# Tying every engine queue of a planned decoder trunk to the order of its own list scheduler

## The chip, the cores and the metric

The kernel runs on one core of one Trainium2 chip. The metric is device time in microseconds (us) of that core, as the median of the runs shown. A core has five engines that each take instructions from a queue of their own, in order: PE (TensorE, matrix products), DVE (VectorE), ACT (ScalarE), POOL (GpSimd) and SP (SyncE, which here only issues DMAs).

## The reference

Two consecutive decoder layers are computed for 256 prompt tokens and 8 sample tokens (one decoding step each), with shared weights in float32. Per layer:

```
u    = rms_norm(x)
proj = u @ w_in                      # columns: attention q,k,v | SSM z,x,B,C,dt | mLSTM q,k,v,o,i,f
att  = sliding-window attention      # window 128, sinks, partial rotary
y    = Mamba-2 SSD scan              # causal conv, chunked scan, gate, grouped norm
h    = mLSTM                         # matrix memory, per-head norm, output gate
x    = x + concat(att, y, h) @ w_out
x    = x + square(relu(rms_norm(x) @ w_up)) @ w_down
```

After both layers there is a final RMSNorm. Besides the two outputs the caches and states of every mixer are returned (the last keys and values, conv rows, SSM states, mLSTM memories). d_model is 2048 and the MLP is 8192 wide.

## The kernel before

**Tiling.** Activations lie transposed: channels on 128 partitions, the 264 tokens along the free axis. Every weight matrix is cut into groups of 128 output columns, and a group into halves of 8 x 128 rows (`half`, line 517). A half is one DMA of 512 KB into `raw` (3 buffers), a rounding to fp32r on ACT (`hi`), the remainder `raw - hi` on DVE (`lo`), and 24 matmuls of 128x264 into a PSUM tile `acc` (2 buffers): 8 times hi by the two parts of the activations (named `uh` and `ul` for the normed input), in two bundles of 8, and then a bundle of 8 lo by `uh`. There are 43 groups for w_in, 32 for w_out (of one half each), 64 for w_up and 64 for w_down in each layer.

**Stages.** A layer first runs the input projection. When a group is complete, DVE takes it out of `acc` (the evacuation) and the mixers' work on it begins: gates, rotary (`rope`, line 680), attention (`att_prompt`, 727), convolution, SSD, the eight SSM states of the samples, mLSTM (`mlstm`, 1059) and the memories of the samples. That work is spread over DVE, ACT, POOL and small matmuls into the PSUM tags `ms` and `sg`, and lies beside the weight halves of later groups. Then w_out and the MLP (`mlp`, 1306) follow, which are nearly nothing but weight halves.

**What sets the order.** The program text does not issue instructions. Each call makes a `Node` (`record`, 191), with a price in us from a formula for each engine (`price`, 228); calls inside `with pr.bundle()` (183) on one engine become a single node. At the end `issue` (258) runs a list scheduler over all nodes. It works out a due time for each node by going backwards (line 282 takes `AHEAD` = 6 us off the due times of weight splits), then moves forward in time: for each engine it looks at the nodes whose inputs are written and whose buffers have room, takes the one that can start first, and among those that can start within 0.08 us the one of the best `rank` (378). On PE small products go before weight bundles. On the others `kind` 0 goes first, which is every node that touches the tags `acc`, `ra` or `ac` (the evacuations and the short chains behind them); the rest go by due time. A node's successor on the same engine counts as ready when the node ends. A load that depends on nothing is held until `EARLY` = 30 us before it is due (289). Where DVE and POOL overlap, the later one is made dearer by 0.6 of the overlap, and of at most its own cost (351). The chosen node is handed on at once by `emit` (383), which takes a physical buffer and calls the real engine method, so that all instructions of the profile carry line 398.

The calls that `emit` makes go to the Tile framework. It adds the waits between engines, and it has a scheduler of its own behind that, which takes the order of the calls as a preference, and need not keep it.

**Places that the prediction speaks of.** In `mlstm` the keys of four heads are turned in one bundle, after the evacuation of four groups by `m_evac` (1046):

```
kp = ms_tile([P, 4, P])
with pr.bundle():
    for h in range(4):
        pe.transpose(kp[:, h], mk[:, h, cs], ident)
```

In `att_prompt` the function `scores` (737) makes one bundle of a mask product and two or four products of `qT` (tag `prod`) with the keys. In `rope` the evacuation into an `ra` tile is followed by a shuffle into an `ac` tile on DVE, two POOL products and a DVE sum. `n0s` (1083) is a small load for the mLSTM of the samples, and `wfin` (1361) holds the gains of the final norm, first used in `last_block` (1339) at the end of the last layer. The stores `C_p` and `n_p` (1116, 1117) follow each other on SP.

Of the kernel before, what the change touches and what calls it, by code (L numbers as in the profile page):

```python
# [32 lines left out]
class Store:  # L33


    def __init__(self, prog, pool, shape, dt, tag, name):
        self.prog, self.pool, self.shape, self.dt, self.tag, self.name = prog, pool, tuple(shape), dt, tag, name
        self.free = int(np.prod(shape[1:]))
        self.real = None
        self.log = []  # L40
        self.users = set()
# [107 lines left out]


_REGIONS = {}


class Node:
# [3 lines left out]
class Program:  # L158
# [4 lines left out]
    EARLY = 30.0  # L163
    LOOSE = ("ms", "sg", "ra", "ac", "eA", "eB")

    def __init__(self, nc):
        self.nc = nc
        self.nodes, self.open, self.tau, self.slots, self.stores = [], None, 0.0, {}, {}
        self.engines = dict(PE=nc.tensor, DVE=nc.vector, ACT=nc.scalar, POOL=nc.gpsimd, SP=nc.sync)
        self.pe, self.vec, self.act, self.pool = [Engine(self, e) for e in ("PE", "DVE", "ACT", "POOL")]  # L170
        self.sync = Engine(self, "SP")
        self.is_weight = False
# [210 lines left out]
    def emit(self, n):  # L383
        for s in n.uses:
            if s.real is not None:
                continue
            slots = self.slots[s.tag]
            k = min((x[1], i) for i, x in enumerate(slots) if x[0] is None)[1]
            slots[k][0], slots[k][1] = s, 0.0
            s.slot = slots[k]  # L390
            s.real = s.pool.tile(list(s.shape), s.dt, name=s.name, tag=f"{s.tag}{k}", bufs=1)
        eng = self.engines[n.eng]

        def real(a):
            return a.real() if isinstance(a, View) else a

        for method, args, kw in n.calls:
            getattr(eng, method)(*[real(a) for a in args], **{k: real(a) for k, a in kw.items()})  # L398


class Engine:
# [9 lines left out]
@with_exitstack  # L411
def trunk(ctx, tc, I, O):
    nc = tc.nc
    pr = Program(nc)
    vec, act, pool, pe, sync = pr.vec, pr.act, pr.pool, pr.pe, pr.sync
    tt, stt, ts = vec.tensor_tensor, vec.scalar_tensor_tensor, vec.tensor_scalar
    ptt = pool.tensor_tensor
# [1095 lines left out]
```

## Time and profile before

| | |
|---|---|
| median of 3 runs | 2429.03 us (2425.24 to 2429.54) |
| profiled execution, its own time | 2427.1 us |
| its span, first to last instruction | 2425.3 us |
| mean granted TensorE clock | 0.985 |
| PE busy | 2341.6 us (97%) |
| DVE busy | 1515.9 us (63%) |
| ACT busy | 1098.1 us (45%) |
| POOL busy | 434.0 us (18%) |
| weight loads | 748 of 512 KB, 3.7 to 3.8 us each to landing |

The busy time of an engine is the union of its instructions, so an engine is idle for the rest of the span. Matmuls overlap one another in the records: one of 128x264 is recorded as about 0.285 us while the next starts 0.12 us after it. A wait is idle time of an engine that a semaphore ended, and it is put down to the instruction that released it. The first layer's mixers lie at about 20 to 372 us, its w_out and MLP up to 1219 us; the second layer's mixers at about 1219 to 1560 us.

### The profile page before, as it was taken

How to read it: one execution, taken by the hardware profiler on the slowest of the kernel's cores; microseconds unless marked ns; L12 is line 12 of the kernel's file. 1: busy time of each engine (PE TensorE's matmuls, PEld its weight loads, DVE VectorE, ACT ScalarE, POOL GpSimd, SP SyncE). 2: the span in 40 equal slices, each digit the busy share in tenths (PEclk: the TensorE clock that was granted, in tenths of full speed). 3: DMA queues.
4: the chain of work that ended last, by engine and by line, in shares of the span. 5: the costliest groups of instructions: out<-in, count | busy, mean ns of one | idle time of the engine just before them, and what ended most of it. 6: DMA issues, size and time to landing. Idle time of an engine off the chain costs nothing.

```text
span 2425.3 us, 46071 instructions
## 1 busy us (share of the span) xinstructions
PE 2341.6 (97%) x18874; PEld 2320.0 (96%) x18874; DVE 1515.9 (63%) x2179; ACT 1098.1 (45%) x1700; POOL 434.0 (18%) x408
## 2 busy tenths in 40 slices
PE   7999898999999999999989979999999999999997
PEld 7998888999999999999989979999999999999997
DVE  7868887754454455455686887977545544544544
ACT  5554444553354344344435544445534434434542
POOL 4314631500000000001331273233000000000023
PEclk9999999999999999999999989999999999999998
DMA  6444755555555555555554466665555555555554
GB/s 235 152 152 139 244 195 166 178 179 183 182 178 182 182 182 180 180 181 182 181 163 128 128 220 178 192 191 182 178 182 180 182 182 178 181 181 183 179 179 131
DMA packets 123475, 432.26 MB, mean 178 GB/s; under 512 B 15744, under 2 KB 18432, under 8 KB 123264
## 3 DMA queue, kind: packets, MB, share of 16 engines
q1 hardware_dynamic: 122688, 428.10, 56.7%
q8 instruction: 149, 2.44, 0.4%
q10 hardware_dynamic: 576, 1.22, 0.1%
q14 instruction: 62, 0.51, 0.1%
HBM read 410.10 MB, written 19.16 MB: 177 GB/s over the span
## 4 chain that ended last, share of the span: by engine, by line
PE 83%; DVE 7%; issue 4%; POOL 3%; DMA 2%; ACT 1%; SPq 0%; DVEq 0%; POOLq 0%; ACTq 0%
PE acc L398 80%; PE ms L398 3%; DVE lo L398 2%; PE sg L398 1%; DMA raw<-in_w_in 1%; DVE m L398 1%; DVE tb L398 1%; POOL S L398 1%; ACT hi L398 1%; POOL tb L398 0%; DMA S<-in_ssm 0%; DVE mw L398 0%; DVE ac L398 0%; POOL ysq L398 0%; DVE lA L398 0%
## 5 line engine op out<-in xcount | busy, mean ns | idle before, releaser
L398 ACT CAST hi<-raw 128x1024 fp32r<-128x1024 f32 x748 | 785.2, 1050 | 1033.7 <-PE acc L398 943.9
L398 DVE TENSOR_TENSOR lo<-raw,hi 128x1024 fp32r<-128x1024 f32 x745 | 949.7, 1275 | 363.9 <-ACT hi L398 359.8
L398 PE MATMUL acc<-uh,hi 128*128 128x264 f32 x3392 | 860.9, 288 | 13.9 <-ACT uh L398 10.3
L398 PE MATMUL acc<-ul,hi 128*128 128x264 f32 x3392 | 854.6, 286 | 2.5 <-DVE ul L398 2.5
L398 PEld LDWEIGHTS acc<-uh,hi 128*128 128x128 f32 x3392 | 643.7, 190 | 15.7 <-ACT uh L398 10.3
L398 PEld LDWEIGHTS acc<-ul,hi 128*128 128x128 f32 x3392 | 645.8, 190 | 5.2 <-DVE ul L398 3.1
L398 PE MATMUL acc<-uh,lo 128*128 128x264 f32 x3392 | 485.6, 286 | 4.5 <-DVE lo L398 4.2
L398 PEld LDWEIGHTS acc<-uh,lo 128*128 128x128 f32 x3392 | 442.9, 189 | 6.4 <-DVE lo L398 5.8
L398 PE MATMUL acc<-hA,hi 128*128 128x264 f32 x1280 | 319.2, 285 | 4.0 <-ACT hA L398 4.0
L398 PE MATMUL acc<-lA,hi 128*128 128x264 f32 x1280 | 319.0, 285 | 0.0
L398 PE MATMUL acc<-hB,hi 128*128 128x264 f32 x1280 | 317.8, 284 | 0.0
L398 PE MATMUL acc<-lB,hi 128*128 128x264 f32 x1280 | 317.6, 284 | 0.0
L398 POOL TENSOR_TENSOR ssq<-xt 128x264 f32<-128x264 f32 x4 | 6.2, 1539 | 1381.4 <-DVE xt L398 1381.4
L398 PEld LDWEIGHTS acc<-hA,hi 128*128 128x128 f32 x1280 | 241.8, 189 | 4.6 <-ACT hA L398 4.3
L398 PEld LDWEIGHTS acc<-lA,hi 128*128 128x128 f32 x1280 | 241.2, 189 | 0.3
L398 PEld LDWEIGHTS acc<-lB,hi 128*128 128x128 f32 x1280 | 241.0, 188 | 0.0
L398 PEld LDWEIGHTS acc<-hB,hi 128*128 128x128 f32 x1280 | 240.8, 188 | 0.0
L398 DVE TENSOR_TENSOR xt<-acc,xt 128x264 f32<-128x264 f32 x192 | 82.9, 432 | 241.9 <-PE acc L398 241.8
L398 PE MATMUL acc<-hA,lo 128*128 128x264 f32 x1280 | 181.0, 283 | 0.0
L398 PE MATMUL acc<-hB,lo 128*128 128x264 f32 x1280 | 180.5, 283 | 0.0
L398 DVE SCALAR_TENSOR_TENSOR ra<-acc,rb 128x264 f32<-128x264 f32 x128 | 55.4, 433 | 197.7 <-PE acc L398 197.6
L398 PEld LDWEIGHTS acc<-hA,lo 128*128 128x128 f32 x1280 | 165.6, 188 | 0.0
(308 smaller groups left out, 1817.5 us busy)
## 6 DMA issues: line engine op xcount, KB each, us to landing
raw<-in_w_up SPq DMA_DIRECT2D x256, 512.0 KB, 3.7
raw<-in_w_down SPq DMA_DIRECT2D x256, 512.0 KB, 3.7
raw<-in_w_in SPq DMA_DIRECT2D x172, 512.0 KB, 3.8
raw<-in_w_out SPq DMA_DIRECT2D x64, 512.0 KB, 3.7
S<-in_ssm SPq DMA_DIRECT2D x16, 512.0 KB, 4.5
out_ssm_s<-S SPq DMA_DIRECT2D x16, 512.0 KB, 3.4
S<-in_mC SPq DMA_DIRECT2D x8, 512.0 KB, 4.6
out_C_s<-S SPq DMA_DIRECT2D x8, 512.0 KB, 3.2
```

Of the source, the lines that this page charges most:

```text
L398: getattr(eng, method)(*[real(a) for a in args], **{k: real(a) for k, a in kw.items()})
```

## The change

Each instruction that `emit` traces gets an edge to the instruction traced before it on the same engine. The edge is of a kind that adds no wait on a semaphore; it only forbids the framework's scheduler to put the two in the other order. Nothing else differs: the nodes, the prices, the list scheduler and its result are those of before.

```diff
+ORDER = mybir.DependencyInfo(mybir.DependencyClass.NoSync, mybir.DependencyReason.DATA)
...
-    def __init__(self, nc):
-        self.nc = nc
+    def __init__(self, tc):
+        self.tc, self.nc = tc, tc.nc
+        nc = tc.nc
+        self.last = {}
...
+        traced = self.nc.cur_bb.bb.instructions
+        at = len(traced)
         for method, args, kw in n.calls:
             getattr(eng, method)(*[real(a) for a in args], **{k: real(a) for k, a in kw.items()})
+        for ins in traced[at:]:
+            before = self.last.get(ins.engine)
+            if before is not None:
+                self.tc.add_manual_dep(ins, before, ORDER, reason="order")
+            self.last[ins.engine] = ins.name
...
-    pr = Program(nc)
+    pr = Program(tc)
```

## Rows read from the trace of the kernel before

**Rows 1.** Page, part 1: busy us, share of the span, instructions.
```profile
PE 2341.6 (97%) x18874; PEld 2320.0 (96%) x18874; DVE 1515.9 (63%) x2179; ACT 1098.1 (45%) x1700; POOL 434.0 (18%) x408
```
**Rows 2.** Windows: length, busy us (instructions) by engine, granted clock, DMA share, GB/s.
```profile
20.00:75.00 55.00, 47.65 (x374) 46.47 (x374) 49.36 (x97) 21.10 (x29) 20.07 (x29) 0.95 0.54 173
...
200.00:285.00 85.00, 74.81 (x555) 72.18 (x554) 78.33 (x85) 37.63 (x111) 62.77 (x27) 0.94 0.62 205
...
472.00:1219.00 747.00, 747.00 (x6143) 746.93 (x6142) 394.56 (x472) 330.89 (x400) 36.04 (x31) 1.00 0.59 181
...
1375.00:1470.00 95.00, 81.55 (x609) 77.83 (x608) 82.91 (x89) 40.14 (x112) 61.93 (x26) 0.93 0.65 206
```
**Rows 3.** Waits of PE over the span: total us, times, longest us.
```profile
PE ms L398 <- DVE m L398: 10.0, 2, 5.8
...
PE sg L398 <- DVE prod L398: 8.2, 3, 4.1
...
PE acc L398 <- DVE m L398: 3.6, 4, 1.0
...
PE ms L398 <- POOL ysq L398: 3.2, 2, 2.7
```
**Rows 4.** Timeline of PE, 1441 to 1448.6: start, us, engine, operation [wait before].
```profile
1441.53 0.29 PE L398 MATMUL acc<-ul,hi 128*128 128x264 f32 x1
1441.66 0.49 PE L398 MATMUL ms<-cst,m 128*128 128x128 f32 x3
1447.98 0.48 PE L398 MATMUL ms<-cst,m 128*128 128x128 f32 x1 [5.83 <-DVE m L398]
1448.11 0.57 PE L398 MATMUL acc<-uh,hi 128*128 128x264 f32 x1
```
**Rows 5.** Timeline of PE, 66.5 to 78.
```profile
67.06 0.83 PE L398 MATMUL sg<-tb,prod 128*128 128x128 f32 x6
71.95 0.79 PE L398 MATMUL sg<-tb,prod 128*128 128x128 f32 x2 [4.06 <-DVE prod L398]
...
77.87 0.42 PE L398 MATMUL acc<-ul,hi 128*128 128x264 f32 x1
```
**Rows 6.** Timeline of SP, 0 to 31: DMA issues.
```profile
11.77 0.33 SPq L398 DMA_DIRECT2D n0s<-in_mn  x1
...
29.78 0.42 SPq L398 DMA_DIRECT2D wfin<-in_wfin  x1
```
**Rows 7.** Timeline of DVE, 66.5 to 72 and, last row, 56.5 to 62.5.
```profile
67.05 0.43 DVE L398 TENSOR_TENSOR ra<-acc,rb 128x264 f32<-128x264 f32 x1
67.40 1.22 DVE L398 TENSOR_TENSOR lo<-raw,hi 128x1024 fp32r<-128x1024 f32 x1
...
68.56 0.44 DVE L398 STREAM_SHUFFLE ac<-ra 128x264 f32<-128x264 f32 x1
...
56.93 1.34 DVE L398 SCALAR_TENSOR_TENSOR m<-m 64x264 f32<-64x264 f32 x3
```
**Rows 8.** Timeline of DVE, 1439 to 1448.
```profile
1439.81 5.92 DVE L398 TENSOR_TENSOR lo<-raw,hi 128x1024 fp32r<-128x1024 f32 x2
...
1447.50 0.42 DVE L398 TENSOR_TENSOR m<-acc,rb 128x264 f32<-128x264 f32 x1
```
**Rows 9.** Timeline of POOL, 1438 to 1449.
```profile
1438.54 3.26 POOL L398 TENSOR_TENSOR S<-S,tb 128x1024 f32<-128x1024 f32 x1
```
**Rows 10.** Groups of DVE in 472:1219, then in 200:372: count, busy us, mean ns, idle before.
```profile
L398 DVE TENSOR_TENSOR lo<-raw,hi 128x1024 fp32r<-128x1024 f32 x256 | 312.3, 1220 | 153.7 <-ACT hi L398 153.7
...
L398 DVE TENSOR_TENSOR lo<-raw,hi 128x1024 fp32r<-128x1024 f32 x41 | 70.1, 1713 | 10.2 <-ACT hi L398 9.8 <-ACT lB L398 0.4
```
**Rows 11.** Timeline of DVE, 1466 to 1483.
```profile
1481.17 1.23 DVE L398 TENSOR_TENSOR lo<-raw,hi 128x1024 fp32r<-128x1024 f32 x1 [7.44 <-ACT hi L398]
```
**Rows 12.** DMA issues of 1440 to 1500: count, KB each, median us to landing.
```profile
out_C_p<-lB SPq DMA_DIRECT2D x1, 256.0 KB, 12.9
out_n_p<-lB SPq DMA_DIRECT2D x1, 2.0 KB, 13.1
```

## The prediction, made before the changed kernel ran

> **What bounds the kernel now.** I read the page's busy times first. PE is busy for 97% of the span [rows 1], and what it is not busy for is 2425.3 - 2341.6 = 83.7 us, some of it ahead of the first matmul and behind the last. Then the windows by stage. In the first MLP, 472 to 1219 us, PE is never idle: 6143 matmuls in 747 us, 0.1216 us each, at the full granted clock [rows 2]. Such a stretch can't gain from another order, and DVE has room in it (395 of 747 us) to keep up with any. So the two MLPs, nearly 1500 us, are fixed, and the change is decided in the mixers. There PE is idle for 7 to 13 us in a window, and DVE is the engine that is nearly full: 49.4 of 55 us, 78.3 of 85, 82.9 of 95 [rows 2]. PE runs dry there because DVE is late with an evacuation, a `lo` or a rotary. Third, the waits of PE name what was late [rows 3], and the timelines of PE and DVE around the longest of them show in what order the queue stood [rows 4, 5, 7, 8].
>
> **Is the planner's order really not the order of before?** Yes, in three places that the code lets one decide. `wfin` is used at the very end; the planner holds a free load until 30 us ahead of its due time, yet SP issues it at 29.8 us, and `n0s` at 11.8 us [rows 6]. A bundle is one node, which the planner starts only when all its inputs are written: the four transposes of `mlstm` stand at 1441.66 with three done, and the fourth waits 5.83 us for an evacuation [rows 4]; `scores` does the same, six matmuls and then 4.06 us [rows 5]. And behind a rotary's evacuation the planner takes the shuffle at once (kind 0, ready when the evacuation ends), yet a `lo` of 1.22 us stands between [rows 7]. I looked at all ten rotaries; none has its shuffle next, and in seven of them it is a `lo` that comes between. So the framework has moved instructions forward in all queues.
>
> **Part by part.** All sums are against the profiled execution's own 2427.1 us (span 2425.3, 1.8 around it); the median of the runs is 1.9 above that.
>
> Broken bundles. Waits inside a bundle are 10.0 us (two transposes of `mlstm`), 8.2 (three `scores`) and 2.7 (the norm sum put into a weight bundle): 20.9 us [rows 3]. With the bundles whole, PE runs weight bundles until the last input is there. It can fill only what it has weights for. At 1441.66 the second `hi` bundle of a half whose first bundle had just run was there [rows 4], and with its `lo` that is 16 x 0.1216 = 1.9 us. If only two of the six places are filled so, the gain is 3.9 us; if all are, 20.9. Most waits are longer than one half, and the planner puts one half behind another, so I take 14.
>
> Clock after the long waits. After the wait in `scores` the matmuls come 0.22 us apart instead of 0.12, recorded with 0.42 us [rows 5]; the granted clock means 0.95, 0.94 and 0.93 in these windows against 1.00 in the MLP, so part of each runs at the lower of the two levels, 1.2 GHz [rows 2]. Ten such matmuls cost 1 us. With four waits of 4 us or more, the bounds are 0 and 6; I take 3.
>
> Evacuations first. PE waited 3.6 us for `m` out of a full `acc` [rows 3]. At 1447.50 the evacuation stands behind two `lo` of 5.92 us together [rows 8]; the planner's rank puts it ahead of every `lo` that has not started. Bounds 0 and 3.6; I take 2. The rotary's chain also becomes 1.2 us shorter [rows 7], which is inside the waits already counted.
>
> Dependent instructions back to back, the price. Between an evacuation and the independent `lo` behind it DVE needs 0.35 us, though the evacuation lasts 0.43; three dependent steps of 0.42 us take 1.34, one each 0.46 [rows 7]. The framework's order often fills that gap, the planner's does not try: 0.11 us for each new dependent pair. The ten rotaries alone give 1.1 us. If a quarter of the mixers' thousand DVE instructions became such pairs, it would be 27 us of DVE time. I take 30 new pairs, 3 us, nearer to the rotaries since the chains of the gates and the convolution already stand largely back to back; it counts in full where DVE is full.
>
> Loads that come later, on SP. The early `n0s` and `wfin` go behind other DMAs. The cover is 30 us against landings of some 13 us at the worst [rows 12]: nothing. If the cover were gone, one landing would show. Where a store stands ahead of a `raw` load in the planner's order, SP waits for its data and all loads behind it wait too; three `raw` buffers are the cover, as before. Bounds -5 and +7 (the two stores below), taken as zero.
>
> The rest of PE's idle time is at most 83.7 - 20.9 - 3.6 = 59 us, start and tail among it. Another order brings these waits, of whole bundles or single matmuls, out longer or shorter; bounds -10 and +10, taken as zero. The edges themselves add no instruction and no wait.
>
> Sum: -14 - 3 - 2 + 3 = -16, so 2411 us in the profiled execution's terms, and 2413 in those of the median. The bounds added up the best way give 2429 - 21 - 6 - 4 - 15 = 2383.
>
> **DVE against POOL.** A `lo` takes 1.22 us in the MLP and 1.71 in the mixers' second half [rows 10]; that excess is 41 x 0.49 = 20 us a layer. The pair at 1439.81 takes 5.92 us [rows 8], and the first of the two starts inside a POOL product that lasts from 1438.54 to 1441.80 [rows 9]. Half of the excess of 5.92 - 2 x 1.22 = 3.48 us is 1.7 us for each. The planner's formula charges at most 0.6 x 1.22 = 0.73. So its order takes a collision for less than half of what it costs. The Trainium skill (SBUF — State Buffer, section "Who interferes with whom") says that a VectorE instruction with two SBUF inputs contends with a GpSimd one that reads SBUF, and that the one issued second stands still until the first is done. The trace agrees in that the `lo` lasts beyond the POOL product. By that rule the order alone decides who pays, and an order that believes in the 0.6 is a way to come out slower; that is the third rival below.
>
> **The rivals.**
> 1. The stalls move and don't go. For it: DVE is busy for nine tenths of the windows where PE waits [rows 2], and work that PE does earlier only brings it sooner to the next evacuation. Against: over the span DVE is at 63% [rows 1], so that the mixers' other windows have DVE time left for work drawn ahead. Time: 2424 to 2434. That the edges do nothing because the queues were already so is in here, and [rows 6] speak against it.
> 2. All goes that order can cause, the waits of whole bundles too: 2383 to 2395, or below. For it: the prices of the plan fit the rows (0.43 for an evacuation, 1.22 for a `lo`, 0.12 for a matmul). Against: DVE's load.
> 3. Slower, by collisions of DVE and POOL in 200 to 285 and 1375 to 1470 us and their like. Each `lo` more that is caught costs 1.7 us of the engine that is the fullest there. The excess of 20 us a layer is about 12 such cases; half as many again in each layer is 12 x 1.7 = 20 us, and 2413 + 20 = 2433; as many again is 2453. It decides from 10 further cases (16 us) on, and with the dependent pairs at twice my value from 8. For it: the planner sees less than half the price. Against: the framework's order is made from the same list, and collides already.
>
> One more thing can go either way. Two stores, `C_p` and `n_p`, take 13 us to land [rows 12], and the loads behind them were late, so that DVE stood for 7.4 us in the second layer [rows 11]. In another order both layers may have that wait, or none: +7 or -7. It widens the range.
>
> **How the numbers follow.** A measurement of this kernel can tell about 0.2% from no change, which is 2424.2 to 2433.9 us. Forecast (2395 to 2424): 0.49. Rival 2: 0.09. Rival 1: 0.15. Rival 3 (2434 to 2455): 0.27. So faster 0.58, same 0.15, slower 0.27. The range from 2383 to 2447 leaves out about 0.05 below and 0.1 above. The likeliest case's own range is 2395 to 2424.
>
> **What would show it.** Right: the MLP windows as before, near 0.1216 us a matmul; the waits inside bundles gone from PE; the shuffle next to its evacuation; `wfin` issued late in the span; the gain in the mixers' windows alone. Wrong: waits of PE for `acc` or `lo` grown by as much as those of bundles fell (rival 1); a mean `lo` above 1.71 us in the mixers' second half (rival 3); the same order as before on SP (no change at all). The forecast fails if PE has no weights to run where it waited, that is, if DVE and not the order kept it idle.

## The result

The changed kernel takes 2389.7 us (median of 4 runs, 2382.85 to 2391.61) against 2428.6 us for the kernel before on the same chip: a ratio of 0.984, interval 0.982 to 0.986. The gain is 39 us where the prediction had 16. The profiled execution of the changed kernel is its fastest one, 2382.85 us with a span of 2381.1, so that its span is 44.2 us shorter than that of before; what follows accounts for those 44.2.

The page's busy times (as [rows 1]) and the mean granted clock, after:

```profile
PE 2324.0 (98%) x18874; PEld 2306.3 (97%) x18874; DVE 1537.6 (65%) x2179; ACT 1098.7 (46%) x1700; POOL 446.3 (19%) x408
```
```profile
core 0: 2381.1 us, clock 0.994
```

PE has as many instructions as before, and is idle 57 us where it was 84. DVE is busier by 21.7 us, which cost nothing. The windows of after that hold nearly the same matmuls as those of [rows 2], in their order from the left (found by counting the products of `lo` with `uh` from the start; columns as there, the first layer's MLP third):

```profile
20.00:67.00 47.00, 46.38 (x373) 45.52 (x372) 43.17 (x69) 18.66 (x21) 20.51 (x25) 1.00 0.62 199
193.00:273.00 80.00, 73.06 (x563) 71.65 (x562) 74.55 (x65) 37.35 (x104) 56.77 (x24) 0.96 0.66 204
458.70:1205.60 746.90, 746.90 (x6142) 746.83 (x6141) 394.63 (x472) 330.72 (x400) 36.38 (x33) 1.00 0.60 183
1349.80:1433.20 83.40, 77.22 (x609) 74.16 (x608) 78.21 (x85) 40.70 (x109) 57.31 (x24) 1.00 0.67 213
```

The MLP is what it was, 746.90 us for 6142 matmuls against 747.00 for 6143. The mixers' windows are shorter by 8.0 of 55, 5.0 of 85 and 11.6 of 95 us, and two of the three now run wholly at the full clock, where they had 0.95 and 0.93. Beside these matmuls DVE now runs 69, 65 and 85 instructions, where it ran 97, 85 and 89: part of its work has moved elsewhere. By the same count PE is 13.4 us ahead at the end of the first layer's mixers and 43.5 us at 1560 us of before: all the gain is in the mixers, 13 us in the first layer and 30 in the second.

PE's waits over the span (as [rows 3]: total us, times, longest):

```profile
PE acc L403 <- ACT uh L403: 9.9, 1, 9.9
PE ms L403 <- POOL ysq L403: 8.8, 1, 8.8
PE sg L403 <- DVE tb L403: 8.1, 8, 1.4
PE ms L403 <- DVE eB L403: 3.5, 2, 1.9
...
PE ms L403 <- DVE m L403: 0.2, 1, 0.2
```

The waits for `m` (10.0 and 3.6) and `prod` (8.2) are gone but for 0.2 us. The wait of 8.8 us for `ysq`, at the end of the first layer's mixers, is no new one: three waits stood at that place before, 3.0 us for `tb`, 4.0 for `hA` and 2.7 for `ysq`. All rows of this view add up to 67.8 us before and 42.0 after. So 26 us of the 44 are waits.

The clock gives most of the rest. A mean of 0.985 over 2425.3 us, with the other level at half speed, is 2 x 0.015 x 2425 = 73 us at 1.2 GHz; 0.994 over 2381.1 is 29 us. That is time at the lower level, not its cost: in both kernels some 14 us of it lie behind the last matmul, and more of it in waits. In the records of the granted clock, 191 matmuls started in the slow stretches before and 54 after. At 0.22 us apart where it is 0.12 at 2.4 GHz, these 137 matmuls are 14 us. 26 + 14 = 40 of 44; the remaining 4 I have not traced. By the page they lie in PE's busy time, which fell by 17.6 us while its idle time fell by 26.6.

What became of [rows 4, 5]: the timeline of PE, the transposes of `mlstm` in the second layer, and the products of `scores`:

```profile
65.37 1.06 PE L403 MATMUL sg<-tb,prod 128*128 128x128 f32 x8
...
1410.38 0.60 PE L403 MATMUL ms<-cst,m 128*128 128x128 f32 x4
1411.79 0.60 PE L403 MATMUL ms<-cst,m 128*128 128x128 f32 x4
```

Eight and four in a row without a wait. What became of [rows 6], the issues on SP:

```profile
11.23 0.33 SPq L403 DMA_DIRECT2D n0s<-in_mn  x1
...
29.61 0.42 SPq L403 DMA_DIRECT2D wfin<-in_wfin  x1
```

Both loads are issued when they were before. Of [rows 7], a rotary on DVE:

```profile
60.75 0.42 DVE L403 TENSOR_TENSOR ra<-acc,rb 128x264 f32<-128x264 f32 x1
...
61.21 0.46 DVE L403 STREAM_SHUFFLE ac<-ra 128x264 f32<-128x264 f32 x1
```

The shuffle now follows its evacuation, in all ten rotaries. And of [rows 10], the groups of `lo` (count, then busy us and mean ns of one) in the MLP and in the mixers' second half, 185 to 360 us:

```profile
L403 DVE TENSOR_TENSOR lo<-raw,hi 128x1024 fp32r<-128x1024 f32 x256 | 312.3, 1220 | 154.9 <-ACT hi L403 154.9
...
L403 DVE TENSOR_TENSOR lo<-raw,hi 128x1024 fp32r<-128x1024 f32 x42 | 70.6, 1685 | 5.3 <-ACT hi L403 4.1 <-PE acc L403 0.7 <-ACT lB L403 0.5
```

1685 ns against 1713: in this stretch DVE and POOL collide as much as before. Over the span all `lo` together took 958.6 us where they took 950.1.

### The profile page after: what moved, and what is told of

Its sections match the earlier page's. It is cut to its first block, busy times and chain, and to the rows that moved or that the text cites. A ratio compares the mean times of both kernels' runs of the same rounds, so it can differ in the third digit from the quotient of the medians.

```text
span 2381.1 us, 46060 instructions
## 1 busy us (share of the span) xinstructions
PE 2324.0 (98%) x18874; PEld 2306.3 (97%) x18874; DVE 1537.6 (65%) x2179; ACT 1098.7 (46%) x1700; POOL 446.3 (19%) x408
## 4 chain that ended last, share of the span: by engine, by line
PE 84%; DVE 3%; DMA 1%; issue 1%; ACT 0%; POOL 0%; DVEq 0%; SPq 0%; ACTq 0%; POOLq 0%
PE acc L403 81%; PE ms L403 2%; DVE lo L403 1%; PE sg L403 1%; DMA raw<-in_w_in 1%; DVE tb L403 0%; ACT hi L403 0%; DVE ra L403 0%; DVE xt L403 0%; DMA out_C_s<-S 0%; DVE ac L403 0%; POOL ysq L403 0%; DVE xs L403 0%; DVE mw L403 0%; ACT eA L403 0%
```

## The experiments

Each kernel is the changed one with the edges kept for some engines or instructions only. The framework decides the order of what is left free anew in each, so that a run shows what is enough, not a pure share. The kernel before took 2425.4, 2425.8, 2426.1 and 2426.4 us on the chips of these runs; ratios are to that. Each text in quotes is what was expected before the run.

| edges on | median us | ratio, interval |
|---|---|---|
| e1: PE | 2426.6 | 1.0006, 0.9996 to 1.0015 |
| e2: DVE | 2407.4 | 0.993, 0.992 to 0.995 |
| e3: ACT, POOL, SP | 2421.1 | 0.998, 0.997 to 0.999 |
| e4: PE, DVE | 2406.4 | 0.992, 0.990 to 0.994 |
| e5: DVE, ACT | 2394.2 | 0.987, 0.986 to 0.989 |
| e6: DVE, SP | 2401.9 | 0.990, 0.989 to 0.992 |
| e7: all but PE | 2387.6 | 0.984, 0.983 to 0.986 |
| e8: all but ACT | 2402.8 | 0.990, 0.989 to 0.992 |
| e9: all but ACT, and on ACT `Bb` and `hi` | 2392.2 | 0.986, 0.984 to 0.988 |
| e10: DVE, evacuations and `lo` alone | 2424.0 | 0.9994, 0.998 to 1.0003 |
| e11: DVE, all but `lo` | 2408.1 | 0.993, 0.991 to 0.994 |
| e13: DVE, nothing earlier | 2413.7 | 0.995, 0.993 to 0.996 |
| e14: DVE, nothing later | 2421.7 | 0.998, 0.998 to 0.999 |
| e12: all, dearer overlap | 2461.4 | 1.014, 1.013 to 1.016 |
| e15: all, factor 0.3 | 2400.7 | 0.991, 0.988 to 0.993 |
| e16: all, factor 1.0 | 2418.7 | 0.997, 0.996 to 0.998 |

### Which engine's order is it?

e1, the prediction's largest term by itself:

```diff
-            if before is not None:
+            if before is not None and n.eng in ("PE",):
```

> Edges on PE's instructions alone, the other four queues left to the framework's scheduler. If the broken bundles carried the gain (the theory of the prediction), this run keeps most of it: 2390 to 2405 us, no wait of PE inside a transpose bundle of mlstm (10.0 us before) or a scores bundle (8.2 us before). If the order on DVE carried it, PE merely waits at the head of the bundle instead of inside it: 2415 to 2430 us, and the waits for m and prod become waits for acc, lo or the same tiles.

Measured: no change. The trace of e1 has the waits that the prediction put on PE's order, and the broken bundle itself. PE's waits, then its timeline:

```profile
PE ms L403 <- DVE m L403: 9.9, 2, 5.8
...
PE sg L403 <- DVE prod L403: 5.8, 2, 3.5
```
```profile
1436.99 0.49 PE L403 MATMUL ms<-cst,m 128*128 128x128 f32 x3
1443.32 0.48 PE L403 MATMUL ms<-cst,m 128*128 128x128 f32 x1 [5.84 <-DVE m L403]
```

PE is bound to the planner's order here and still stops between the third and the fourth transpose. The bundle is whole in the queue, and here its fourth instruction waited by itself: PE started the bundle when its turn had come, and stopped where an input was late. The cause is what made the input late.

e2, e3 and e4 (the same line with other engines):

```diff
+            if before is not None and n.eng in ("DVE",):
```


> Edges on DVE's instructions alone. If the order on DVE carried the gain (evacuations and the rotary's chain first), 2390 to 2405 us, with the shuffle right behind its evacuation and PE's waits for m, prod, lo gone. If the broken bundles on PE carried it, 2415 to 2430 us, with the waits inside bundles still there.


```diff
+            if before is not None and n.eng in ("ACT", "POOL", "SP"):
```


> Edges on ACT, POOL and SP alone, PE and DVE left to the framework. Both theories above: 2420 to 2432 us, since neither needs these queues. A third theory, that the loads and stores of SP or the roundings on ACT stood in the wrong place, gives under 2415 us here.


```diff
+            if before is not None and n.eng in ("PE", "DVE"):
```


> Edges on PE and DVE, the other three left to the framework. If these two queues carry the gain, 2386 to 2394 us, as with all edges; if ACT, POOL or SP have a share of their own, over 2398 us.

DVE's edges alone give 18 us, ACT, POOL and SP without DVE 4, and PE adds nothing to DVE (1 us, inside the intervals). e2 lies between its two ranges. 18 + 4 is 22 of 39: some of the gain needs DVE and another engine together. e5 to e8 ask which:

```diff
+            if before is not None and n.eng in ("DVE", "ACT"):
```


> Edges on DVE and ACT. Theory: ACT is the second queue, since with DVE alone bound ACT stands 27 us in 200 to 285 us and 24 us in 1383 to 1475 us at the copy Bb, which waits for POOL to have read the last Bb, and the hi roundings queue behind it, so that DVE waits 12 and 18 us for hi. With ACT bound too these waits go: 2387 to 2395 us, ACT's wait for POOL tb under 5 us in each of the two stretches. If SP or POOL hold the rest: 2403 to 2408 us, as with DVE alone or DVE and PE.


```diff
+            if before is not None and n.eng in ("DVE", "SP"):
```


> Edges on DVE and SP. By the ACT theory 2403 to 2408 us, as with DVE alone (2407.4). If the loads and stores of SP in the planner's order hold the rest of the gain, 2387 to 2397 us.


```diff
+            if before is not None and n.eng in ("DVE", "ACT", "POOL", "SP"):
```


> Edges on DVE, ACT, POOL and SP, PE left to the framework. PE's edges alone changed nothing, so 2387 to 2393 us, the time of all edges; if PE's order matters once the other queues are right, 2396 us or more. With PE's queue free the bundles can be broken here.


```diff
+            if before is not None and n.eng in ("PE", "DVE", "POOL", "SP"):
```


> Edges on PE, DVE, POOL and SP, ACT left to the framework. By the ACT theory most of the second half of the gain is lost: 2400 to 2408 us. If any three queues besides DVE do as well, 2388 to 2395 us.

ACT is worth 13 us once DVE is bound (2407.4 to 2394.2; and 2402.8 to 2389.7 from the other side), SP 5.5 (2407.4 to 2401.9, between e6's two ranges), SP and POOL together 6.6 beside DVE and ACT (2394.2 to 2387.6), and PE nothing again: without its edges the kernel is as fast as with all of them. POOL's edges were not run by themselves.

### What ACT's order does

In e8 ACT is free. Its timeline, then DVE's:

```profile
253.67 0.37 ACT L403 COPY Bb<-sg 128x256 f32<-128x256 f32 x1 [5.96 <-POOL tb L403]
253.94 2.00 ACT L403 CAST hi<-raw 128x1024 fp32r<-128x1024 f32 x2
```
```profile
255.02 1.23 DVE L403 TENSOR_TENSOR lo<-raw,hi 128x1024 fp32r<-128x1024 f32 x1 [5.64 <-ACT hi L403]
```

`Bb` (in the loop over the samples' SSM states) has one buffer, and POOL is still reading it. ACT stands at that copy for 5.96 us, two roundings stand behind it in the queue, and DVE waits 5.64 us for the first of them. e9 binds these and nothing else of ACT:

```diff
-        for ins in traced[at:]:
-            ...
+        tags = {v.tag for v in n.uses}
+        if n.eng != "ACT" or tags & {"Bb", "hi"}:
+            for ins in traced[at:]:
+                ...
```


> DVE, POOL, PE and SP have all their edges; on ACT only the eight copies Bb of the samples, the two Bb of the norm and the roundings hi are tied to one another, everything else on ACT is free to be moved. Theory (ACT's share of the gain is the roundings that the framework left behind a copy Bb, which has to wait for POOL): the time falls from the 2402.8 us of all edges but ACT's to 2386 to 2393 us, PE's clock records and DVE's waits for ACT hi in the samples' windows are those of the changed kernel (2 to 3 us where 12 and 18 us were). Rival (ACT's share is spread over its whole order): 2400 to 2405 us, and DVE still waits over 10 us for ACT hi there.

Measured 2392.2, so 10.6 of ACT's 13 us. ACT's waits at `Bb` for POOL and DVE's for `hi` between 160 and 300 us (total us, times, longest), in e8, then DVE's in e9:

```profile
ACT Bb L403 <- POOL tb L403: 26.8, 6, 6.0
...
DVE lo L403 <- ACT hi L403: 15.9, 9, 5.6
```
```profile
DVE lo L403 <- ACT hi L403: 6.0, 5, 2.7
```

In e9 ACT has no wait for POOL's `tb` there at all: the planner puts the roundings ahead of a copy that can't start yet. In the trace of before the same wait is 17.5 us, four times:

```profile
ACT Bb L398 <- POOL tb L398: 17.5, 4, 5.3
```

Over the whole span this wait is 30.1 us before and 58.6 us in e2: with DVE alone bound it grew. So ACT's 13 us are what its order is worth beside a bound DVE; how much of them the kernel before lost is not shown.

### What DVE's order does

The prediction's reading was that an evacuation stood behind `lo` that the framework had put there. e10 ties only evacuations and `lo` to one another, e11 everything on DVE but `lo`:

```diff
+        if n.eng == "DVE" and tags & {"acc", "lo"}:
...
```


> Edges on DVE alone, and there only between the instructions that read acc (the evacuations) and the remainders lo; every other DVE instruction is free. With all of DVE's edges the time was 2407.4 us, with none 2425.4. Theory (DVE's share is that an evacuation no longer stands behind a lo): 2406 to 2413 us, PE's waits for DVE m out of acc and inside the transposes gone. Rival (the share comes from the order of the many small instructions of rotary, gates and norms): 2420 to 2427 us.


```diff
+        if n.eng == "DVE" and "lo" not in tags:
...
```


> Edges on DVE alone, between all its instructions except the remainders lo, which stay free to be moved between the others. Theory (an evacuation behind a lo is what cost): 2418 to 2427 us, as without edges. Rival (the small instructions' order): 2405 to 2412 us, as with all of DVE's edges.

The rival was right: e10 gives nothing and e11 all of DVE's 18 us. Compared as sequences, the evacuations and `lo` of before stand in the planner's order at all but 19 of 1173 places. The place of [rows 8], in e10 with that order bound:

```profile
1434.61 5.92 DVE L403 TENSOR_TENSOR lo<-raw,hi 128x1024 fp32r<-128x1024 f32 x2
...
1442.30 0.42 DVE L403 TENSOR_TENSOR m<-acc,rb 128x264 f32<-128x264 f32 x1
```

The two `lo` of 5.92 us are the planner's own. What the framework moves is the rest: of DVE's 996 other instructions, 361 stand earlier in the order of before than in the planned one, which is the order of after, counted in evacuations and `lo` (up to 57 places), and 47 later (1 to 3 places). Ahead of the evacuation at 1447.50 of [rows 8] are nine such. The timeline of DVE in the kernel before, then in after that evacuation and some of the nine:

```profile
1431.96 0.85 DVE L398 SCALAR_TENSOR_TENSOR xs<-xs,vec,ms 128x128 f32<-128x128 f32 x3
1432.73 0.68 DVE L398 TENSOR_TENSOR hB<-ms,q2c 128x512 f32<-128x512 f32 x1
1433.33 0.52 DVE L398 TENSOR_TENSOR kws<-m,EG 128x32 f32<-128x32 f32 x1
...
1435.25 1.21 DVE L398 TENSOR_TENSOR tb<-S,sg 128x1024 f32<-128x1024 f32 x1
1436.50 0.69 DVE L398 TENSOR_REDUCE CS<-tb 128x4 f32<-128x512 f32 x1
...
1445.65 1.21 DVE L398 TENSOR_TENSOR tb<-S,sg 128x1024 f32<-128x1024 f32 x1
1446.90 0.69 DVE L398 TENSOR_REDUCE CS<-tb 128x4 f32<-128x512 f32 x1
```
```profile
1409.60 0.43 DVE L403 TENSOR_TENSOR m<-acc,rb 128x264 f32<-128x264 f32 x1
...
1413.66 1.20 DVE L403 TENSOR_TENSOR tb<-S,sg 128x1024 f32<-128x1024 f32 x1
...
1423.27 0.35 DVE L403 TENSOR_TENSOR kws<-m,EG 128x32 f32<-128x32 f32 x1
...
1425.38 1.21 DVE L403 TENSOR_TENSOR tb<-S,sg 128x1024 f32<-128x1024 f32 x1
1426.63 0.69 DVE L403 TENSOR_REDUCE CS<-tb 128x4 f32<-128x512 f32 x1
```

From their start to that of the next evacuation or `lo`, the three groups of before took 1.82, 1.85 and 1.85 us, 5.5 in all. PE's wait for this evacuation was 5.83 us [rows 4]. e13 forbids coming forward and e14 slipping back:

```diff
...
+        if n.eng == "DVE":
+            anchor = bool({v.tag for v in n.uses} & {"acc", "lo"})
+            for ins in traced[at:]:
+                before = self.last.get("anchor")
+                if before is not None:
+                    self.tc.add_manual_dep(ins, before, ORDER, reason="order")
+                if anchor:
+                    self.last["anchor"] = ins.name
```


> Edges on DVE alone: the evacuations and lo in their planned order among themselves, and every other instruction tied behind the last evacuation or lo that the planner put ahead of it. So it can't come forward past one; it may slip back, and the others are free among themselves. Theory (small instructions brought forward are what cost): 2404 to 2411 us, as with all of DVE's edges (2407.4), and PE's waits for DVE m in the transposes and for prod gone. Rival (their order among themselves, or those moved back): 2418 to 2427 us.


```diff
...
+                if anchor:
+                    for before in self.last.get("group", []):
+                        self.tc.add_manual_dep(ins, before, ORDER, reason="order")
+                    self.last["group"] = [ins.name]
+                else:
+                    self.last.setdefault("group", []).append(ins.name)
```


> The mirror of the run before: evacuations and lo in their planned order, each tied behind all other DVE instructions that the planner put ahead of it. So none can slip back past one, and all may come forward. Theory (coming forward costs): 2420 to 2428 us, as without edges, and PE's wait for DVE m in the transposes still 5 to 6 us. Rival: 2404 to 2412 us.

e13 is 12.7 us faster than before, e14 4.7. e13 lies between its two ranges; e14 lies in the first of its own, but a little below the kernel before, by more than its interval. So coming forward is about two thirds of DVE's share, and 5 us hang on the rest. The waits are clearer than the times. In e13 no wait of PE for `m` or `prod` is left, and the evacuation waits for PE where PE had waited for it (timeline of DVE):

```profile
1425.13 0.85 DVE L403 SCALAR_TENSOR_TENSOR xs<-xs,vec,ms 128x128 f32<-128x128 f32 x3
1427.43 0.43 DVE L403 TENSOR_TENSOR m<-acc,rb 128x264 f32<-128x264 f32 x1 [1.45 <-PE acc L403]
```

In e14 the break is where it was (timeline of PE):

```profile
1435.27 0.49 PE L403 MATMUL ms<-cst,m 128*128 128x128 f32 x3
1441.59 0.47 PE L403 MATMUL ms<-cst,m 128*128 128x128 f32 x1 [5.83 <-DVE m L403]
```

So the waits for `m` and `prod` of [rows 3] come from small DVE instructions that were ready early and were taken early, in front of evacuations and `lo` that PE needed sooner. Half of the 361 last under 0.42 us, and all but 11 under 1.3 us.

In one of the waits for `m` the way is longer. The kernel before at that place (timeline of all engines), then the same store in after (timeline of SP):

```profile
1465.75 0.58 SPq L398 DMA_DIRECT2D out_C_p<-lB  x1
...
1480.09 1.04 ACT L398 CAST hi<-raw 128x1024 fp32r<-128x1024 f32 x1 [6.57 <-DMA raw<-in_w_in]
...
1482.80 0.33 PE L398 MATMUL ms<-cst,m 128*128 128x128 f32 x1 [4.12 <-DVE m L398]
```
```profile
1494.48 0.58 SPq L403 DMA_DIRECT2D out_C_p<-lB  x1
```

The evacuation that PE waited for stood behind the `lo` of [rows 11], that `lo` behind a rounding, and the rounding 6.57 us for a weight load that SP issued behind the store `C_p` (437 weight loads were ahead of the store). The store waits for four DVE instructions on `lB`, and the last of them stands 30 evacuations and `lo` earlier in before than in the plan. In e1, e10 and e14, where these DVE instructions may still come forward and SP is free, the store also follows 437 loads, and a wait of 4.0 to 6.1 us stands at this place. In after and in the other runs with the same plan it follows 457. The longest wait of DVE for `hi` in the second layer is then at most 5.0 us, where it was 7.3 to 9.6.

e13's time is 6 us above e2's. Other waits of PE are longer there, 58.3 us in all against 54.6, and 181 matmuls started at the lower clock against 154. At 0.1 us each these are 3.7 and 2.7 us of the 8.5 between their profiled spans. Why the free order of the small instructions came out worse there is not shown.

### The price of an overlap

Rival 3 rested on the planner charging too little for a DVE instruction caught by POOL. e12 charges all that is left of the other instruction; e15 and e16 change the factor alone:

```diff
-                n.cost += 0.6 * min(n.cost, max(0.0, port["POOL" if e == "DVE" else "DVE"] - s))
+                n.cost += max(0.0, port["POOL" if e == "DVE" else "DVE"] - s)
```


> All edges, and the planner charges an instruction of DVE or POOL that starts inside one of the other with all that is left of it, where it charged 0.6 of that and at most 0.6 of the instruction's own cost. If the underpriced collisions still cost the changed kernel time (a lo takes 1.69 us in the mixers' second half against 1.22 in the MLP, some 20 us of DVE a layer): 2372 to 2384 us, and a mean lo there under 1.6 us. Rival (no order avoids them, or they lie beside other work by now): 2385 to 2395 us, and a mean lo as it was.


```diff
+                n.cost += 0.3 * min(n.cost, max(0.0, port["POOL" if e == "DVE" else "DVE"] - s))
```


> All edges, and the planner's factor for a DVE-POOL overlap 0.3 where it was 0.6. If the planner's spreading of DVE and POOL work costs more than the collisions (as the run with the dearer price says, 72 us slower at a mean lo of 1.54 us in the mixers' second half), a cheaper price is faster still: 2365 to 2385 us, with a mean lo above 1.6 us there. If 0.6 stands near the best: 2385 to 2410 us.


```diff
+                n.cost += 1.0 * min(n.cost, max(0.0, port["POOL" if e == "DVE" else "DVE"] - s))
```


> All edges, and the factor 1.0, still with no more than the instruction's own cost charged for an overlap. If time rises with the price: 2400 to 2440 us, between the changed kernel and the dearer price (2461). If the dearer price's loss came from charging more than the instruction's own cost: 2383 to 2395 us.

2400.7, 2389.7, 2418.7 and 2461.4 us for 0.3, 0.6, 1.0 and the whole remainder. e12 lies far outside both of its ranges, yet it did what was asked of it: fewer collisions. The mean `lo` in the mixers' second half, the window of that half, and PE's waits:

```profile
L403 DVE TENSOR_TENSOR lo<-raw,hi 128x1024 fp32r<-128x1024 f32 x43 | 65.7, 1538 | 8.1 <-ACT hi L403 7.7 <-issue 0.3
```
```profile
200.00:380.00 180.00, 151.34 (x1115) 143.79 (x1114) 144.46 (x208) 78.28 (x217) 79.35 (x45) 0.89 0.54 177
```
```profile
PE sg L403 <- DVE tb L403: 26.3, 13, 8.8
PE ms L403 <- POOL ysq L403: 17.7, 2, 8.8
PE acc L403 <- DVE ra L403: 16.6, 7, 7.0
```

43 x (1.685 - 1.538) = 6 us of `lo` were saved in that layer, and DVE is busy for only 144 of 180 us, where after has 153 of 166 (193.0 to 358.7 us): the planner lets DVE and POOL stand rather than overlap, and PE waits for both. By this planner a collision costs less than its avoidance. Each price makes another plan, so the 11 us between 0.3 and 0.6 say no more than that none of the other three prices is better. No kernel of these is faster than the changed one by more than the intervals.

## Why the prediction was wrong

The size failed above all in one term: the clock, taken at -3 with a bound of -6, gave -14. The mechanism failed in the largest term: it was to come from PE's queue, and PE's edges gave nothing; DVE's gave 18 us, and ACT's 13 beside them. The terms of the sum, by the profiled spans:

| term | taken | measured |
|---|---|---|
| broken bundles | -14 | -18.0 (`m` and `prod`) |
| clock after long waits | -3 | -14 |
| evacuations first | -2 | -3.6 |
| dependent pairs | +3 | none seen in the time |
| the rest and SP | 0 | -4 of waits, -4 not traced |
| sum | -16 | -44 |

**What held.** The MLP unchanged at 0.1216 us a matmul, the gain in the mixers alone, the shuffle next to its evacuation, and the waits for `m` and `prod` gone. 2389.7 us lies in the range, and in rival 2's 2383 to 2395 us, which had 0.09. Rival 2's ground, that the prices of the plan fit, was not tested.

**The evidence for the moved order.** Of the three places, one stands. `wfin` at 29.8 us is the planner's own choice, since it is issued at 29.6 us with all edges. Line 277 of the kernel before caps a due time at 60 us after the node's place in the program, `wfin` is called at the start (line 1361), and 30 us ahead of 60 is 30. The broken bundles are no moved order on PE (e1); only the rotary of [rows 7] was one. The conclusion was right with two wrong reasons under it, which was luck.

**Broken bundles, -14: near in size, wrong in engine.** `m` and `prod` gave 18 us of 18.2. The third wait of this term, `ysq`, did not go: with the two waits ahead of it, it was 9.7 us and is 8.8 after. The step took a wait between two instructions of one bundle for a sign that PE's queue had been reordered, and argued from what PE could run instead. PE's edges are worth 0 (e1, e4, e7). What made the input late was the thing to look at: [rows 8] was read as two `lo` in front, and the nine small instructions around them were passed over.

**Clock, -3 with a bound of -6: it gave 14.** This is the term that was most mis-sized. The step allowed for a stretch of slow matmuls behind each of four long waits. But 191 matmuls started in the slow stretches, 19 us that were at stake. The records have eleven such stretches before and four after, the last of each behind the last matmul. Of the ten others before, nine lie at or just behind waits of 1.8 to 5.8 us, so that shorter waits than the four longest had one too, and one (1322.6 to 1329.5 us) lies at no wait.

**Evacuations first, -2 with a bound of -3.6.** The waits for `m` out of a full `acc` went from 3.6 to nothing, but not because an evacuation passed a `lo` (e10).

**The rest, taken as zero within 10.** It gave 4 us of waits (26 - 18.0 - 3.6), inside the bound: those for ACT's `lA` (4.6) and for `lo` (4.2) are gone from the list of after, and others have grown. The wait for `lA` had ACT's queue behind it: ACT stood 4.72 us at a `Bb` copy shortly ahead, with two roundings behind it. The prediction named queue effects on SP and DVE and never looked at ACT's own waits, where 30.1 us for `Bb` stood. Binding those copies and the roundings is worth 11 us once the other queues are bound (e9). These 11 us show in PE's waits and slow matmuls, and are no further term of the sum.

**Loads on SP, zero within -5 and +7.** SP's edges gave 5.5 us beside DVE's (e6); which of its loads or stores does that is not shown. Of the two cases that the prediction left open for the stores, "none" came: the wait of 7.4 us of [rows 11] is gone, and PE's 4.12 us behind it, which are counted above under `m`. Either engine's order was enough to end the 7.4 us: they are gone in e2 with SP free, and in e3 with DVE free. The longest wait of DVE for `hi` is now 3.0 us.

**Dependent pairs, +3.** The pitch from an evacuation to its shuffle is 0.46 us (60.75 to 61.21) against 0.35 with an independent successor, as supposed. DVE's busy time rose by 21.7 us, of which 15.8 are instructions that lasted longer (8.5 of it `lo`). It did not reach the end of the kernel, because DVE was late by its order and not by its load.

**Rival 3, 0.27.** The mean `lo` did not rise (1685 against 1713 ns). The Trainium skill (SBUF — State Buffer, section "Who interferes with whom") says that such a `lo`, with two inputs in SBUF, contends with a GpSimd instruction that reads SBUF. The trace agrees: a `lo` takes 1685 ns in the mixers' second half and 1220 in the MLP. But the step from there to a slower kernel needed more collisions, and an order that is bound to a plan had about as many as one that was not. Rival 1 put DVE's load against a gain; DVE at nine tenths of a window was no bound, as more than a third of its small instructions stood ahead of their turn.

## What to carry to other kernels

A wait between two instructions of a group that the program keeps together says that an input was late, not that the waiting engine's queue was reordered. Follow the releaser, and list everything that stands ahead of it on its own engine, the small instructions as well as the large; if it waited too, follow that on, here once as far as a load behind a store. On each engine look for an instruction that stands waiting for a buffer with urgent work queued behind it. And when waits of a PE-bound kernel are counted, count the matmuls that start at the lower clock too: here they gave more than half as much again as the waits themselves.

## What the runs showed of the hardware

The granted clock is the part that I had not expected in this size. Before, 0.985 on the span, after 0.994, and with the dearer price, where PE waits longer and oftener (94 us in all rows of its waits), 0.975, which is 123 us at 1.2 GHz. In this kernel 26 us of waits less came with 14 us of faster matmuls. The two do not go in step: e13, with 9.5 us of waits less, is at 0.986 and has 181 matmuls at the lower clock where before had 191, while e2, with 13.2 us less, has 154.
